# A list schedule that counts pauses on TensorE and moves 65 short runs of operations by a table

## The chip, the cores and the metric

One core of one Trainium2 chip runs the whole program. The metric is device microseconds of one execution, launch to last output; the profiler's span runs from the first to the last instruction and is a little shorter. The engines are TensorE (PE, with its weight loads as PEld), VectorE (DVE), ScalarE (ACT), GpSimd (POOL) and SyncE (SP), which here issues the weight transfers.

## What is computed

Two layers over 256 tokens of width 1024, float32 in and out, with 16 heads of 64 in 4 key groups. Each layer normalizes `x`, scales and shifts it by numbers that come from `c` through `ada_w`, runs a mixer and adds the gated result. Cut to what matters:

```
cond = silu(c)
for i in range(2):
    shift, scale, gate = split(cond @ ada_w[i] + ada_b[i], 3)
    h = rms_norm(x, norm_g[i]) * (1 + scale) + shift
    # i = 0: q, kc, vc, ks, vs, kw, vw, gates, z from h @ nsa_w_in; rms_norm and rope on q and k;
    #   p_cmp (15 compressed blocks: gelu(blocks @ cmp_w1 + b1) @ cmp_w2), p_slc, p_win (256 keys): softmax(q k) v,
    #   o = g0 * o_cmp + g1 * o_slc + g2 * o_win;  y = (o * silu(z)) @ nsa_w_out
    # i = 1: q, k, v, z from h @ moba_w_in; one causal block of 256 keys: o = softmax(q k) v
    #   y = (o * silu(z)) @ moba_w_out
    x = x + gate * y
```

## The kernel before

The program isn't issued as it is written. `T`, `A`, `V`, `G` and `S` stand for TensorE, ScalarE, VectorE, GpSimd and SyncE; every call on them is recorded by `Plan.record` with a number (its id, 2530 of them), an estimated cost (`_cost`), the operations it depends on and the buffers that it needs. At the end `Plan.issue` is a list scheduler: it keeps a clock for each engine, looks at the operations that are ready, takes the one that can start first, among equals the one of the lowest level (`FIRST_OF_ALL`, `URGENT`, `CHAIN`, `FILL`), then the one with the lowest id, and emits it. So the order on each engine, and which buffer of a tag (`ps`, `raw`, `hi`, `lo`, `p` and so on) a tile gets, are what the planner's model makes of it. Each engine then runs its own list strictly in order and waits for semaphores; the planner's clock has no part in the run itself. Since all operations are emitted from one line, nearly every row of the profile says L373 (L403 in the changed kernel), and rows are told apart by the names of their tiles.

The stages, with the times of the profile:

- To about 55 us: `condz` times `ada_w` (tiles `early`, later `raw`) gives scale and shift, columns of `h` are built (`HT`, a high and a low part in fp32r) and the key and value columns are multiplied (`acc`, `ps`).
- A weight piece of 512 KB (`raw`) is loaded by SP, cast on ACT to `hi` and subtracted on DVE to `lo`; each product is three matmuls, `hi,HT`, `lo,HT`, `hi,HT`.
- To about 100 us: query columns, the layer's gate logits (`tiny<-acc,GBIAS`, `gates`), rope on keys (`n_out`, `rot`, then `y<-n_out` and transposes `ps<-identF,y` into `KTA`), the compression (`ps<-p,p`). The z columns follow (`acc<-HT,hi`), and between them `condz` products of later `ada_w` pieces (`ps<-raw,condz`).
- 103 to 190 us: eight head pairs (`pair_a`): scores `ps<-KTA,qg`, masked maximum on DVE (`p<-ps,causal`), exponentials on ACT (`p<-p,tiny`), scaling on DVE, transposes `ps<-identF,p`, ACT copies to `pT`, values `ps<-pT,VA`, gating (`g<-zT,ps`, `qg<-g`).
- 180 to 210 us: the out projection (`hi,qg`, `lo,qg`), `x` updated, and `next_h`: sum of squares, reciprocal root (`rs`), `n_in<-X,rs`, transposes `ps<-identF,n_in`, `n_out<-ps,AB`, `HT`. The first weights of layer 1 go to `KTA`, `n_parts` and `qg` (`first_parts`).
- 210 to 258 us: layer 1's columns. To 300 us: its eight pairs (`pair_b`), among them the matmuls of the out projection. To 312 us: the rest of that projection, then the update of `x` and the output.

Groups with a `tile_position` (`values`, `ps<-p,p`, `ps<-raw,condz`) use parts of the array side by side; they are called tiled below, and a stretch of them with other matmuls on both sides is an excursion.

## Time and profile before

| | |
|---|---|
| median of 3 runs (lowest, highest) | 317.1 us (315.71, 317.89) |
| the profiled execution, its span | 317.45 us, 315.7 us |
| PE, PEld busy | 306.0 us (97%), 243.5 us (77%) |
| DVE, ACT, POOL busy | 242.2, 205.0, 26.6 us |
| DMA | 65.82 MB, mean 208 GB/s |

A row of the timeline gives the start, the time from first start to last end, engine, line, operation, output and inputs, the tile's size, how many equal instructions in a row were merged, and in brackets idle time and its releaser. Matmuls overlap, so the pace of PE is read from start to start, and a wait that is shorter than a matmul's tail shows no idle time. A row of the waits gives the waiting instruction, what it waited for, the sum, the count and the longest. A row of the stretches gives busy microseconds and instruction counts of PE, PEld, DVE, ACT and POOL, then granted clock, DMA share and GB/s.

### The profile page before, as it was taken

How to read it: one execution, taken by the hardware profiler on the slowest of the kernel's cores; microseconds unless marked ns; L12 is line 12 of the kernel's file. 1: busy time of each engine (PE TensorE's matmuls, PEld its weight loads, DVE VectorE, ACT ScalarE, POOL GpSimd, SP SyncE). 2: the span in 40 equal slices, each digit the busy share in tenths (PEclk: the TensorE clock that was granted, in tenths of full speed). 3: DMA queues.
4: the chain of work that ended last, by engine and by line, in shares of the span. 5: the costliest groups of instructions: out<-in, count | busy, mean ns of one | idle time of the engine just before them, and what ended most of it. 6: DMA issues, size and time to landing. Idle time of an engine off the chain costs nothing.

```text
span 315.7 us, 6158 instructions
## 1 busy us (share of the span) xinstructions
PE 306.0 (97%) x2133; PEld 243.5 (77%) x2133; DVE 242.2 (77%) x734; ACT 205.0 (65%) x486; POOL 26.6 (8%) x102
## 2 busy tenths in 40 slices
PE   4999999998999999999999999999999999999995
PEld 4666677777766797858879888877788999968784
DVE  4673374669982899835979887998599999999764
ACT  5735155764835787456799966786486489998420
POOL 8248900000000000000000000000000000000000
PEclk9999999999999999999999999999999999999999
DMA  7999999359899822788272377617188862423102
GB/s 248 320 357 367 368 359 323 111 171 311 279 309 306 277 79 90 246 304 250 113 261 76 116 217 226 240 60 212 65 261 263 298 229 84 155 69 120 59 34 102
DMA packets 44174, 65.82 MB, mean 208 GB/s; under 512 B 4221, under 2 KB 20971, under 8 KB 44142
## 3 DMA queue, kind: packets, MB, share of 16 engines
q1 hardware_dynamic: 43782, 65.36, 63.1%
q8 instruction: 17, 0.28, 0.4%
q14 instruction: 15, 0.12, 0.1%
q10 hardware_dynamic: 168, 0.06, 0.1%
q0 software_dynamic: 192, 0.00, 0.0%
HBM read 64.36 MB, written 1.05 MB: 207 GB/s over the span
## 4 chain that ended last, share of the span: by engine, by line
PE 90%; DMA 5%; ACT 2%; DVE 1%; issue 1%; SPq 0%; ACTq 0%; DVEq 0%
PE ps L373 54%; PE acc L373 36%; DMA raw<-in_nsa_w_in_dram 2%; DMA early<-in_ada_w_dram 2%; ACT hi L373 1%; DMA rot<-in_c_dram 0%; ACT n_in L373 0%; DVE lo L373 0%; DVE p L373 0%; ACT p L373 0%; DVE AB L373 0%; ACT HT L373 0%; DVE rot L373 0%; DVE y L373 0%; DVE X L373 0%
## 5 line engine op out<-in xcount | busy, mean ns | idle before, releaser
L373 ACT CAST hi<-raw 128x1024 fp32r<-128x1024 f32 (+1 forms) x48 | 48.8, 1023 | 25.5 <-DMA raw<-in_nsa_w_in_dram 9.8
L373 DVE TENSOR_TENSOR lo<-raw,hi 128x1024 fp32r<-128x1024 f32 (+1 forms) x48 | 56.4, 1181 | 11.0 <-ACT hi L373 10.8
L373 PE MATMUL acc<-hi,HT 128*128 128x512 f32 (+1 forms) x160 | 49.6, 381 | 1.3 <-ACT n_in L373 0.8
L373 ACT ACTIVATE p<-p,tiny 128x128 f32<-128x128 f32 (+1 forms) x96 | 43.2, 460 | 8.4 <-DVE tiny L373 8.3
L373 PE MATMUL acc<-HT,hi 128*128 128x256 f32 x192 | 37.8, 286 | 0.0
L373 PEld LDWEIGHTS acc<-hi,HT 128*128 128x128 f32 x160 | 29.1, 188 | 9.6 <-issue 2.9
L373 DVE CUSTOM_DVE_ANT_0 p<-ps,causal 128x128 f32<-128x128 f32 (+1 forms) x96 | 30.5, 346 | 3.1 <-PE ps L373 3.1
L373 PEld LDWEIGHTS acc<-HT,hi 128*128 128x128 f32 x192 | 30.1, 188 | 0.8 <-issue 0.7
L373 PE MATMUL acc<-lo,HT 128*128 128x512 f32 (+1 forms) x80 | 30.2, 380 | 0.2 <-DVE lo L373 0.2
L373 PE MATMUL ps<-hi,HT 128*128 128x512 f32 (+1 forms) x96 | 28.2, 365 | 0.0
L373 PE MATMUL acc<-HT,lo 128*128 128x256 f32 x96 | 27.8, 290 | 0.0
L373 PE MATMUL ps<-KTA,qg 128*128 128x256 f32 (+2 forms) x192 | 27.0, 284 | 0.0
L373 ACT COPY pT<-ps 128x384 f32<-128x384 f32 x48 | 21.5, 485 | 6.3 <-PE ps L373 6.2
L373 PEld LDWEIGHTS ps<-KTA,qg 128*128 128x128 f32 x192 | 24.2, 190 | 1.7 <-issue 1.2
L373 PE MATMUL ps<-hi,qg 128*128 128x256 f32 (+1 forms) x96 | 24.1, 323 | 0.0
L373 PE MATMUL acc<-hi,qg 128*128 128x512 f32 x64 | 22.8, 402 | 0.0
L373 PE MATMUL ps<-identF,p 128*128 128x128 f32 x144 | 21.7, 276 | 0.0
L373 PEld LDWEIGHTS ps<-hi,HT 128*128 128x128 f32 x96 | 17.0, 188 | 4.2 <-issue 2.1
L373 PEld LDWEIGHTS ps<-identF,p 128*128 128x128 f32 x144 | 16.4, 140 | 3.9 <-issue 1.2
L373 ACT ACTIVATION_READ_ACCUMULATOR p<-p,tiny 128x1 f32 x96 | 19.3, 201 | 0.0
L373 PE MATMUL ps<-pT,VA 128*64 128x256 f32 (+1 forms) x192 | 19.1, 334 | 0.0
L373 PEld LDWEIGHTS acc<-HT,lo 128*128 128x128 f32 x96 | 18.1, 189 | 0.1
(223 smaller groups left out, 614.5 us busy)
## 6 DMA issues: line engine op xcount, KB each, us to landing
raw<-in_ada_w_dram SPq DMA_DIRECT2D x32, 512.0 KB, 4.9
raw<-in_moba_w_in_dram SPq DMA_DIRECT2D x20, 512.0 KB, 4.3
early<-in_ada_w_dram SPq DMA_DIRECT2D x12, 512.0 KB, 9.5
raw<-in_nsa_w_in_dram SPq DMA_DIRECT2D x12, 512.0 KB, 6.4
early<-in_nsa_w_in_dram SPq DMA_DIRECT2D x9, 512.0 KB, 9.1
p<-in_nsa_cmp_w_dram SPq DMA_DIRECT2D x16, 256.0 KB, 3.8
raw<-in_nsa_w_out_dram SPq DMA_DIRECT2D x8, 512.0 KB, 5.7
raw<-in_moba_w_out_dram SPq DMA_DIRECT2D x8, 512.0 KB, 4.8
```

What stands on the lines that cost most here:

```text
L373: r = getattr(self.engines[e], method)(*[self._real(a) for a in args], **{k: self._real(a) for k, a in kw.items()})
```

## The change

Nothing of what is computed changes: the same operations are recorded with the same dependencies. What changes is the planner.

- A TensorE operation that crosses a multiple of `TICK` (10240/3 ns on the planner's clock) costs `PAUSE`, 93 ns, more.
- `_cost` counts tiled matmuls by rows as well as columns, and adds 100 ns where fewer than 128 rows are used.
- `HOLD` gives 8 ids an earliest time on the planner's clock.
- `LATER_BY` adds a number to 65 ranges of ids; the sum replaces the id as the last criterion.
- An operation that needs several new tiles of one tag is considered only when they are free together.

```
+TILED, LATER, PAUSE = -0.5, 0, 93.0
+LATER_BY = [
+    (385, 385, -73), (401, 403, 93), (413, 413, -223), (420, 422, 40), (456, 456, 66), (463, 463, -169),
...
+    (2394, 2395, -77), (2401, 2401, -45), (2407, 2407, 352),
+]
+SHIFT = {i: d for a, b, d in LATER_BY for i in range(a, b + 1)}
+HOLD = {
+    2: 800, 48: 7000, 90: 12000, 124: 17600, 247: 15900, 688: 109200, 1642: 209100, 1665: 215200,
+}
...
-                m = free(aps[1])
-                if "tile_position" in kw and m <= 64:
-                    return max(cols * 4.28 * max(32, m) / P, 60.0)
+                m, rows = free(aps[1]), aps[1].shape[0]
+                if "tile_position" in kw and m * rows <= 64 * P:
+                    return max(cols * 4.28 * max(32, m) / P * max(32, rows) / P, 60.0) + (100.0 if rows < P else 0.0)
...
-            op["at"] = 0.0
+            op["at"], op["key"] = HOLD.get(op["id"], 0.0), op["id"] + SHIFT.get(op["id"], 0)
...
+                    new = {}
+                    for n in op["needs"]:
+                        if self.tiles[n]["slot"] is None:
+                            new.setdefault(self.tiles[n]["tag"].name, []).append(n)
+                    for name, several in new.items():
+                        if len(several) > 1 and not blocked:
+                            free = sorted(self.tags[name].free)
+                            blocked = len(free) < len(several)
+                            t = t if blocked else max(t, free[len(several) - 1][0])
...
-                    found.append((t, self._rank(op, e, mode), op["id"], op))
+                    found.append((t, self._rank(op, e, mode), op["key"], op))
...
+                if (start + cost) // TICK > tick:
+                    cost += PAUSE
```

The orders that come out differ nearly everywhere: 871 of TensorE's 1278 operations stand at another place (by up to 89 places), 476 of VectorE's 638, 272 of ScalarE's 387, 40 of SyncE's 155 transfers (by up to 5), none of GpSimd's. The last 64 operations of TensorE, after 300 us, are in the old order. TensorE has 36 excursions before and 31 after. Three places, with the rows of the program's order:

**At 76 to 82 us, ScalarE and VectorE.** `n_in<-acc` copies the query columns, `tiny<-acc,GBIAS` the gate logits of the same accumulator; `hi`, `lo` are weight parts; `n_out`, `y` belong to the rope on keys. ScalarE before, then after:

```order
L373 COPY n_in_176<-acc_276 128x256
L373 ACTIVATE tiny_907<-tiny_907 128x48
L373 COPY n_in_176<-acc_283 128x256
L373 CAST hi_352<-raw_640 128x1024
L373 COPY y_143<-n_out_279 128x512
L373 COPY y_217<-n_out_279 128x512
L373 ACTIVATE tiny_925<-tiny_925 128x48
L373 ACTIVATE n_out_286<-n_in_176 128x1024
```

```order
L403 COPY n_in_182<-acc_276 128x256
L403 COPY n_in_182<-acc_288 128x256
L403 ACTIVATE tiny_911<-tiny_911 128x48
L403 ACTIVATE tiny_915<-tiny_915 128x48
L403 ACTIVATE n_out_286<-n_in_182 128x1024
L403 CAST hi_302<-raw_622 128x1024
L403 COPY y_143<-n_out_279 128x512
L403 COPY y_208<-n_out_279 128x512
```

A little ahead, at 66 to 73 us, VectorE before, then after; `lo` of 608 columns belongs to the query weights, and SP's next loads of `raw` wait for these rows:

```order
L373 TENSOR_TENSOR lo_315<-raw_625,hi_309 128x608
L373 TENSOR_REDUCE ss_819<-n_out_279 128x16
L373 TENSOR_TENSOR lo_346<-raw_640,hi_334 128x608
L373 TENSOR_SCALAR rs_834<-ss_819 128x16
L373 TENSOR_TENSOR lo_368<-raw_647,hi_352 128x608
```

```order
L403 TENSOR_TENSOR lo_369<-raw_622,hi_345 128x608
L403 TENSOR_TENSOR lo_349<-raw_636,hi_334 128x608
L403 TENSOR_REDUCE ss_835<-n_out_279 128x16
L403 TENSOR_TENSOR lo_271<-raw_644,hi_302 128x608
L403 TENSOR_SCALAR rs_853<-ss_835 128x16
```

VectorE at 75 to 79 us, before, then after:

```order
L373 TENSOR_TENSOR n_out_279<-n_in_164,TC 128x1024
L373 TENSOR_TENSOR rot_139<-n_in_164,TS 128x16x8 x2
L373 TENSOR_TENSOR tiny_907<-acc_276,GBIAS 128x48
L373 TENSOR_TENSOR lo_315<-raw_618,hi_309 128x1024
L373 TENSOR_TENSOR n_out_279<-n_out_279,rot_139 128x16x16
```

```order
L403 TENSOR_TENSOR lo_369<-raw_636,hi_345 128x1024
L403 TENSOR_TENSOR rot_140<-n_in_164,TS 128x16x8
L403 TENSOR_TENSOR tiny_911<-acc_276,GBIAS 128x48
L403 TENSOR_TENSOR rot_140<-n_in_164,TS 128x16x8
L403 TENSOR_TENSOR tiny_915<-acc_288,GBIAS 128x48
L403 TENSOR_TENSOR n_out_279<-n_in_164,TC 128x1024
```

At 66 us the second `lo` moves ahead of the reduction `ss` (on ScalarE the squares `n_out<-n_in` that it reads move behind the second cast); the third stays behind it. Later the weight part `lo` moves ahead of the gate logits and the rope product `n_out` behind them; on ScalarE the two copies `y` move from ahead of the large `n_out` to behind it, and a cast stays ahead of them.

**At 199 to 207 us, TensorE and ScalarE: the end of the first out projection and `next_h`.** ScalarE before, then after:

```order
L373 CAST hi_251<-raw_625 128x1024
L373 CAST hi_309<-raw_618 128x1024
L373 CAST hi_334<-raw_647 128x1024
L373 ACTIVATE n_in_176<-X,rs_834 128x256
L373 ACTIVATE n_out_286<-ps_162,AB_119 128x128
L373 ACTIVATE n_in_176<-X,rs_834 128x256
L373 CAST HT<-n_out_286 128x2x128
```

```order
L403 CAST hi_302<-raw_657 128x1024
L403 CAST hi_334<-raw_644 128x1024
L403 ACTIVATE n_in_182<-X,rs_853 128x256 x3
L403 ACTIVATE n_out_286<-ps_213,AB_119 128x128
L403 ACTIVATE n_out_286<-ps_162,AB_119 128x128
L403 CAST HT<-n_out_286 128x2x128 x2
```

TensorE before, then after:

```order
L373 MATMUL ps_162<-identF,n_in_176 128x128 x2
L373 MATMUL ps_212<-hi_352,qg_1448 128x512
L373 MATMUL ps_212<-lo_368,qg_1448 128x512
L373 MATMUL ps_196<-identF,n_in_176 128x128 x2
L373 MATMUL ps_212<-hi_352,qg_1448 128x512
L373 MATMUL ps_224<-identF,n_in_176 128x128 x2
L373 MATMUL acc_276<-KTA,HT 128x512 x2
```

```order
L403 MATMUL ps_213<-identF,n_in_182 128x128 x2
L403 MATMUL ps_162<-identF,n_in_182 128x128 x2
L403 MATMUL ps_233<-identF,n_in_182 128x128 x2
L403 MATMUL ps_190<-identF,n_in_182 128x128 x2
L403 MATMUL acc_276<-hi_345,qg_1504 128x512 x2
L403 MATMUL acc_276<-lo_369,qg_1504 128x512
L403 MATMUL acc_276<-hi_345,qg_1504 128x512
L403 MATMUL acc_288<-KTA,HT 128x512 x12
```

One of the three casts is no longer ahead of `n_in<-X,rs`, the three `n_in` stand together, and so do the four pairs of transposes that read them, now ahead of four matmuls of the out projection. On VectorE the subtraction `n_parts<-raw,n_parts` no longer stands between the two additions `ss<-ss` that open `next_h`.

**At 281 to 298 us, TensorE: the pairs of layer 1.** `ps<-pT,VA` is a tiled group of four calls (eight matmuls of the profile), one for each pair. Before, one of them stands between matmuls of the out projection; after, three stand in one stretch:

```order
L373 MATMUL ps_224<-hi_309,qg_1464 128x512
L373 MATMUL ps_156<-pT_1389,VA 64x256
L373 MATMUL ps_156<-pT_1275,VA 64x256
L373 MATMUL ps_156<-pT_1389,VA 64x128
L373 MATMUL ps_156<-pT_1275,VA 64x128
L373 MATMUL ps_224<-hi_309,qg_1464 128x512
```

```order
L403 MATMUL ps_233<-lo_310,qg_1510 128x512
L403 MATMUL ps_162<-pT_1275,VA 64x256
L403 MATMUL ps_162<-pT_1261,VA 64x256
...
L403 MATMUL ps_190<-pT_1239,VA 64x256
L403 MATMUL ps_190<-pT_1311,VA 64x256
...
L403 MATMUL ps_162<-pT_1269,VA 64x256
L403 MATMUL ps_162<-pT_1261,VA 64x256
...
L403 MATMUL ps_247<-KTA,qg_1545 128x256 x4
```

Further down two more groups come together, and around 272 us another two.

More of the change, by code (lines that the diff above doesn't have):

```diff
@@ L37 @@
 DEEP = 2e4
-TILED, LATER = -0.5, 0
+TILED, LATER, PAUSE = -0.5, 0, 93.0
 SHORT_ROWS, SMALL, BEHIND, EARLY_RATE = 1.1, 7e4, 5500.0, 348.0
 ISSUE, FIRST_BYTE, RATE, LANDED = 450.0, 1500.0, 315.0, 700.0
+LATER_BY = [
[12 rows of a table added]
+]
[3 more added lines that the diff above has]
+}
 class Tag:
```

10 rows, old and new, of the table LATER_BY are left out of this document.

## The prediction

> **What bounds the kernel.** I read the page first, then the waits of TensorE, then its timeline. The page:
>
> ```profile
> PE 306.0 (97%) x2133; PEld 243.5 (77%) x2133; DVE 242.2 (77%) x734; ACT 205.0 (65%) x486; POOL 26.6 (8%) x102
> PEclk9999999999999999999999999999999999999999
> PE 90%; DMA 5%; ACT 2%; DVE 1%; issue 1%; SPq 0%; ACTq 0%; DVEq 0%
> ```
>
> TensorE is busy for 97% of the span at the full granted clock, and 90% of the chain that ended last is its own. Of the waits of TensorE, three of the five longest (between the first two stands one for `x` itself):
>
> ```profile
> PE ps L373 <- POOL selP L512: 2.3, 1, 2.3
> ...
> PE acc L373 <- ACT n_in L373: 0.8, 1, 0.8
> ...
> PE ps L373 <- DVE p L373: 0.3, 1, 0.3
> ```
>
> The first and the one for `x` belong to the start, which the change hardly touches. The others shown are 1.1 us, and since a wait hides in the tail of the matmul before it, I add those that show only as a late start (below). An order of the same work can gain two things: these waits, and what TensorE loses where the kind of matmul changes. The pauses that the planner now counts come first, in a stretch of one kind:
>
> ```profile
> 228.38 0.62 PE L373 MATMUL acc<-hi,HT 128*128 128x512 f32 x2
> 229.07 0.62 PE L373 MATMUL acc<-hi,HT 128*128 128x512 f32 x2
> ...
> 234.56 0.62 PE L373 MATMUL acc<-hi,HT 128*128 128x512 f32 x2
> ```
>
> From 228.38 to 234.56 there are nine steps of three matmuls (one `lo,HT` stands between the rows). The first takes 0.69 us, and all nine take 6.18, 0.687 each. A pause of 93 ns every 3.41 us would fall on one or two of the nine and make the mean 0.01 to 0.02 longer than an undisturbed step; the first is no shorter than the mean. So counting pauses by itself is worth nothing here. Whatever the planner makes of them only reshuffles, and the time must come from the new places.
>
> [...]
>
> **Excursions.** A values group among matmuls of 512 columns:
>
> ```profile
> 288.69 0.40 PE L373 MATMUL ps<-hi,qg 128*128 128x512 f32 x1
> 289.02 0.87 PE L373 MATMUL ps<-pT,VA 128*64 128x256 f32 x8
> 289.82 0.50 PE L373 MATMUL ps<-hi,qg 128*128 128x512 f32 x1
> 290.16 0.39 PE L373 MATMUL ps<-lo,qg 128*128 128x512 f32 x1
> ```
>
> A plain step is 0.229 us (0.687 / 3 above). The step into the group (288.69 to 289.02) takes 0.33, the step after it (289.82 to 290.16) 0.34: 0.21 us for one excursion. The order has 31 instead of 36, so 5 x 0.21 = 1.05 us of TensorE work goes: one at 15 us, one around 272, three between 285 and 298. Only the last four, 0.85 us, can reach the end. The first dies at the wait that comes next.
>
> **66 to 82 us.** The longest wait after the start, in the chain in order of time, with VectorE's rows ahead of it:
>
> ```profile
> 70.08 6.94 DMA raw<-in_nsa_w_in_dram
> 77.12 1.05 ACT hi L373
> ...
> 78.49 1.65 PE acc L373 x6
> ```
>
> ```profile
> 67.99 1.22 DVE L373 TENSOR_REDUCE ss<-n_out 128x16 f32<-128x1024 f32 x1 [1.23 <-ACT n_out L373]
> 69.13 0.78 DVE L373 TENSOR_TENSOR lo<-raw,hi 128x608 fp32r<-128x608 f32 x1
> 69.91 0.79 DVE L373 TENSOR_TENSOR lo<-raw,hi 128x608 fp32r<-128x608 f32 x1
> ```
>
> The second of three loads is issued at 70.08, lands at 77.02, its cast holds ScalarE to 78.17, and only then comes the copy that frees the accumulator. TensorE waits 0.82 us. Whatever it gains before (the 0.3 us on `p`, the excursion at 15 us) ends in this wait unless the load comes earlier. After the change two things pull against each other. The first load's buffer is free earlier (its `lo` now precedes the reduction). The second load's comes later: its `lo` stands behind the reduction, whose input moved behind the second cast and a copy on ScalarE. Those two are short pieces; a cast of 1024 columns takes 1.05 us by the row at 77.12, these of 608 and 512 together about 1.2. So it ends near 71.9 instead of 70.7, and the issue slips from 70.08 by about 1.8 us. The first load then has the engines to itself and lands earlier, and 6.94 us was a load among others. The bounds for the landing are the old length, 71.9 + 6.9 = 78.8 (1.8 us late), and the page's median for loads of this size in a calmer stage:
>
> ```profile
> raw<-in_moba_w_in_dram SPq DMA_DIRECT2D x20, 512.0 KB, 4.3
> ```
>
> That is 76.2, 0.8 us early, which is about all that TensorE has to wait here. Behind it stands one thing more: the gate logits ran at 76.92 on VectorE, ahead of that copy; now `lo` (1.22 us) precedes them and they read the bank after the copy, 0.3 us later. I take 78.3 for the accumulator, 0.2 earlier than now. Then the two `y<-n_out`, behind the large `n_out` (1.05) and a cast (1.05), end near 81.7, when TensorE arrives at the transposes that read them, 78.3 + 8 x 0.23 + 1.2 for a compression pair + 0.2 = 81.6. That costs 0.1. Sum to 82 us: **-0.1**, with -0.8 and +1.8 as ends.
>
> **105 and 122 us.** The same kind of `condz` group twice:
>
> ```profile
> 105.02 1.32 PE L373 MATMUL ps<-raw,condz 128*32 128x512 f32 x8
> 106.27 0.44 PE L373 MATMUL ps<-identF,g 128*128 128x128 f32 x2
> ...
> 121.61 1.07 PE L373 MATMUL ps<-raw,condz 128*32 128x512 f32 x8
> 122.61 0.33 PE L373 MATMUL ps<-identR,n_parts 64*128 64x64 f32 x2
> ```
>
> From start to next start the first took 1.25 us, the second 1.00. I take it that the first ran while its weights were landing; it now stands directly ahead of the second, over 6 us later: **-0.25**, and nothing if the load wasn't the cause. The number of excursions stays (two groups leave a compression pair and join each other).
>
> **199 to 208 us.** ScalarE, then VectorE, then TensorE:
>
> ```profile
> 201.20 0.19 ACT L373 ACTIVATION_READ_ACCUMULATOR y<-X 128x1 f32 x1
> ...
> 204.01 1.05 ACT L373 CAST hi<-raw 128x1024 fp32r<-128x1024 f32 x1 [0.35 <-PE ps L373]
> 204.97 0.51 ACT L373 ACTIVATE n_in<-X,rs 128x256 f32<-128x256 f32 x1
> ```
>
> ```profile
> 200.77 1.22 DVE L373 TENSOR_TENSOR n_parts<-raw,n_parts 128x1024 fp32r<-128x1024 f32 x1
> 201.91 0.15 DVE L373 TENSOR_TENSOR ss<-ss 128x1 f32<-128x1 f32 x1
> ```
>
> ```profile
> 205.53 0.44 PE L373 MATMUL ps<-identF,n_in 128*128 128x128 f32 x2 [0.16 <-ACT n_in L373]
> 206.58 0.74 PE L373 MATMUL acc<-KTA,HT 128*128 128x512 f32 x2
> ```
>
> The chain of `next_h` loses two obstacles. `n_parts` no longer holds the second addition; that one then waits only for ScalarE's sum, ending at 201.39, and starts about 0.35 earlier. And the cast at 204.01 no longer stands ahead of `n_in`, so that `n_in` starts near 203.6 instead of 204.97. The first `acc<-KTA,HT` waits for the `HT` of the first chunk, which I find at 206.2 with four transposes done instead of three (0.2 us of work): 206.58 + 0.2 - 206.2 = 0.58 earlier. What is late next: ScalarE's queue of `n_out<-ps` and `HT`, and the second half's `n_in` near 214, where I count 0.1 back. **-0.5**, ends 0 and -0.8. Weight loads were also exchanged here (the first weights of layer 1 ahead of the last out weights); at my placing the last out piece is converted some 0.5 us ahead of its use, so a slip of a load there would take this term away.
>
> **240 to 300 us.** Busy time by stretch:
>
> ```profile
> 270.00:280.00 10.00, 10.00 (x82) 8.58 (x81) 9.66 (x37) 9.50 (x29) 0.00 (x0) 1.00 0.45 157
> 280.00:290.00 10.00, 10.00 (x69) 7.12 (x68) 10.00 (x41) 10.00 (x38) 0.00 (x0) 1.00 0.18 59
> 290.00:300.00 10.00, 10.00 (x66) 7.85 (x67) 7.81 (x21) 4.98 (x10) 0.00 (x0) 1.00 0.30 101
> ```
>
> VectorE works 9.66 and 10.00 of 10 us, ScalarE 9.50 and 10.00, and TensorE never waits: all three are full. Saved excursions count only if VectorE's work ahead of a values group shrinks as well. VectorE's groups from 255 to 300 us:
>
> ```profile
> L373 DVE CUSTOM_DVE_ANT_0 p<-ps,causal 128x128 f32<-128x128 f32 (+1 forms) x32 | 10.1, 345 | 0.0
> L373 DVE TENSOR_SCALAR p<-p,tiny 128x128 f32<-128x128 f32 (+1 forms) x32 | 8.2, 310 | 0.0
> L373 DVE SCALAR_TENSOR_TENSOR g<-zT,ps 128x256 f32<-128x256 f32 x8 | 3.3, 414 | 0.7 <-PE ps L373 0.7
> ```
>
> Against what VectorE had done by 284 us, its list ahead of the stretch of three groups has four maxima (`p<-ps,causal`) and seven scalings (`p<-p,tiny`) more, and six maxima, six scalings, a `g<-zT,ps` and its `qg` less. At 0.345, 0.31 and 0.41 us that is 3.6 more and 4.7 less: about 1 us shorter. So of the 0.85 us I take **-0.6**, ends 0 and -0.85. What moved behind fits where VectorE has 2.2 us to spare, 290 to 300.
>
> [...]
>
> **The sum.** -0.1 - 0.25 - 0.5 - 0.6 = -1.45. The profiled execution took 317.45 us (span 315.7), 0.35 above the median of 317.1. So 316.0 against its own time, and **315.7** against the median. Waits of 0.1 or less I leave as they are.
>
> **Rivals.** *The waits go in full.* The loads at 70 us land in about 4 us: 0.8 there, the whole 0.85 of excursions, 0.25, 0.8, and late starts that show elsewhere, such as this pair of the compression:
>
> ```profile
> 101.19 1.62 PE L373 MATMUL ps<-p,p 128*64 128x256 f32 x8
> 102.74 0.38 PE L373 MATMUL acc<-HT,hi 128*128 128x256 f32 x1
> ...
> 104.00 1.08 PE L373 MATMUL ps<-p,p 128*64 128x256 f32 x8
> ```
>
> It took 1.55 us, the next, up to 105.02, 1.02: 0.5 more. 317.1 - 3.2 = 313.9 at least, and 313.4 with a few like it. For it speaks that no engine but TensorE is full before 240 us, against it the VectorE rows.
>
> *VectorE holds the merged values groups back* (slower). Three groups in one stretch need the probabilities of three pairs, so two pairs' scalings, maxima and exponentials are wanted up to 11 us earlier. If what was put off doesn't make room, because it is needed to free `ps` or `p`, TensorE stands for those 3.6 us: 317.1 - 0.85 (the other terms) + 3.6 = 319.8. It decides from the point where VectorE's list ahead of these groups is longer than before; I count it 1 us shorter, which speaks against it.
>
> *The table's gains are the planner's alone.* Pauses that don't exist were planned around, the load at 70 us still rules, and the rest cancels: 317.1, no change.
>
> **Chances.** Forecast (314.3 to 316.6) 0.45, no change 0.22, waits in full 0.23, VectorE 0.10. I take over 1%, about what a measurement of this kernel tells from no change, as the line: faster 0.23, within it 0.67, slower 0.10. The range leaves out a tenth on either side: from 313.1, below the first rival's centre, to 318.6, which holds the +1.8 end at 78 us with the other terms at half or less.
>
> **What would show it.** A start at or below 78.3 us of the first 512-column `acc<-hi,HT` behind the 304-column ones; groups of `ps<-raw,condz` of 1.0 us at 112 us; `acc<-KTA,HT` 0.5 us earlier relative to what precedes it; 31 excursions at 0.21; no wait on VectorE in the stretch of three groups. A late landing at 77 us, or a wait on `p` or `ps` over 1 us near 285, would make it wrong.

## The result, and the profile after

The changed kernel takes **318.78 us** in the median (317.49 to 321.55), the kernel before 316.68 beside it: a ratio of **1.0071 [1.005, 1.0091]**. It is slower by 2.1 us, where 315.7 (313.1 to 318.6) was forecast, 1.45 us faster than the profiled execution of before. One of the twenty executions of before was a slow one (376.84 us) and is left out of the ratio. The profiled execution of after took 318.79 us, its span 317.1. From its page:

```profile
PE 304.9 (96%) x2133; PEld 243.6 (77%) x2133; DVE 242.6 (77%) x734; ACT 204.5 (65%) x486; POOL 28.9 (9%) x102
PEclk9999999999999999999999999999999999999999
PE 79%; DVE 8%; DMA 6%; issue 2%; ACT 2%; SPq 1%; ACTq 0%; DVEq 0%
```

TensorE is busy 1.1 us less than before, but its share of the chain that ended last falls from 90% to 79%; VectorE's grows from 1% to 8%. Four of the waits of TensorE (sum, count, longest):

```profile
PE acc L403 <- DVE tiny L403: 2.1, 1, 2.1
...
PE ps L403 <- DMA early<-in_ada_w_dram: 0.9, 2, 0.7
PE ps L403 <- DVE p L403: 0.6, 1, 0.6
PE ps L403 <- DVE n_parts L403: 0.6, 1, 0.6
```

The first stands where 0.8 us stood for `n_in`; those on `early` and `n_parts` are new, the one on `p` was 0.3. To see where the time goes I read the start of TensorE's next matmul at points where both kernels have done exactly the same work (named by the time in before; "start" is the 69th matmul):

| work done | start | 57 | 90 | 180 | 213 | 223 | 300 | last matmul |
|---|---|---|---|---|---|---|---|---|
| before | 12.93 | 56.98 | 89.65 | 180.41 | 212.83 | 223.47 | 300.29 | 311.89 |
| after | 13.39 | 56.94 | 91.59 | 182.72 | 214.56 | 224.84 | 301.68 | 313.24 |

These two executions differ by 1.35 us, less than the medians do: the one profiled of before is a late one (317.45 against 316.68), and up to 180 us profiles of the same order scatter by about a microsecond in each stretch. So I take the stretches from the profiles of all kernels below that carry the one or the other order there:

| stretch (us) | old order: mean (lowest, highest, n) | new order | difference |
|---|---|---|---|
| 0 to 57 | 56.88 (56.64, 57.22, 12) | 57.34 (56.92, 57.95, 6) | +0.46 |
| 57 to 90 | 32.73 (32.11, 33.41, 9) | 33.73 (33.05, 34.65, 4) | +1.00 |
| 90 to 180 | 90.26 (89.94, 90.76, 11) | 91.86 (91.11, 93.61, 7) | +1.60 |
| 180 to 213 | 32.41 (32.37, 32.42, 4) | 31.82 (31.79, 31.84, 5) | -0.59 |
| 213 to 223 | 10.64 (10.63, 10.64, 4) | 10.27 (10.26, 10.28, 5) | -0.37 |
| 223 to 300 | 76.83 (76.82, 76.84, 4) | 76.84 in four of five, 77.72 in one | 0 |
| 300 to the end | 11.60 (11.59, 11.60, 4) | 11.55 (11.55, 11.56, 5) | -0.05 |

The sum is +2.05 us (0.65%), which is what the medians show. The loss is made before 180 us, the gains behind it. In the three stretches ahead of 180 us the profiles of one order scatter by 0.6 to 2.5 us, so there the differences are means with a wide margin; behind 180 us they are sharp.

**66 to 80 us.** The chain of after in order of time (start, length):

```profile
67.44 3.93 DMA raw<-in_nsa_w_in_dram
...
72.22 6.36 DMA raw<-in_nsa_w_in_dram
...
78.68 1.04 ACT hi L403
79.72 0.28 ACT n_in L403
...
80.03 0.22 DVE tiny L403
...
80.29 0.73 PE acc L403 x2
```

The second load is issued at 72.22 (70.08 before), takes 6.36 us and holds ScalarE until 79.72; TensorE starts at 80.29 instead of 78.49, with 2.1 us of idle time. A part of it begins earlier, on SP's queue, first before and then after:

```profile
61.87 0.37 SPq L373 DMA_DIRECT2D raw<-in_ada_w_dram  x1
```

```profile
65.24 0.37 SPq L403 DMA_DIRECT2D raw<-in_ada_w_dram  x1
```

This load waits for a buffer that frees 3.4 us later: the subtraction `lo<-raw,hi` on VectorE that reads the buffer now stands behind four copies `p<-ps` that it stood ahead of, and runs at 64.36 instead of 61.05. Why the planner put it there isn't shown.

**256 us.** VectorE and TensorE of before, then of after:

```profile
255.23 1.28 DVE L373 TENSOR_TENSOR n_parts<-n_out,n_parts 128x512 fp32r<-128x512 f32 x2
...
255.97 1.56 PE L373 MATMUL ps<-identR,n_parts 128*128 128x128 f32 x16
```

```profile
254.75 1.22 DVE L403 TENSOR_TENSOR lo<-raw,hi 128x1024 fp32r<-128x1024 f32 x1
255.88 1.28 DVE L403 TENSOR_TENSOR n_parts<-n_out,n_parts 128x512 fp32r<-128x512 f32 x2
...
256.62 0.89 PE L403 MATMUL ps<-identR,n_parts 128*128 128x128 f32 x8 [0.62 <-DVE n_parts L403]
```

A weight part (`lo`) now stands ahead of `n_parts` on VectorE, and the group that reads it starts 0.65 us later. That takes back what the merged value groups gain behind it.

### The profile page after: what moved, and what is told of

It is laid out like the page before. It is cut to its first block, busy times and chain, and to the rows that moved or that the text cites. A ratio compares the mean times of both kernels' runs of the same rounds, so it can differ in the third digit from the quotient of the medians.

```text
span 317.1 us, 6164 instructions
## 1 busy us (share of the span) xinstructions
PE 304.9 (96%) x2133; PEld 243.6 (77%) x2133; DVE 242.6 (77%) x734; ACT 204.5 (65%) x486; POOL 28.9 (9%) x102
## 3 DMA queue, kind: packets, MB, share of 16 engines
HBM read 64.36 MB, written 1.05 MB: 206 GB/s over the span
## 4 chain that ended last, share of the span: by engine, by line
PE 79%; DVE 8%; DMA 6%; issue 2%; ACT 2%; SPq 1%; ACTq 0%; DVEq 0%
PE ps L403 48%; PE acc L403 31%; DMA raw<-in_nsa_w_in_dram 3%; DVE lo L403 3%; DMA y<-in_ada_b_dram 2%; DMA early<-in_ada_w_dram 1%; ACT hi L403 1%; DVE n_out L403 1%; DVE ss L403 1%; DVE gate L403 1%; SPq L403 1%; DVE rs L403 1%; DVE rot L403 1%; DVE p L403 1%; DVE KTA L403 0%
## 5 line engine op out<-in xcount | busy, mean ns | idle before, releaser
L403 ACT ACTIVATE p<-p,tiny 128x256 f32<-128x256 f32 (+1 forms) x96 | 42.7, 450 | 5.5 <-DVE tiny L403 5.4
L403 PE MATMUL acc<-HT,hi 128*128 128x256 f32 x192 | 39.3, 290 | 0.0
L403 DVE CUSTOM_DVE_ANT_0 p<-ps,causal 128x256 f32<-128x256 f32 (+1 forms) x96 | 30.1, 348 | 5.6 <-PE ps L403 4.9
L403 PE MATMUL ps<-KTA,qg 128*128 128x256 f32 (+2 forms) x192 | 27.8, 285 | 0.0
L403 PE MATMUL ps<-hi,qg 128*128 128x256 f32 (+1 forms) x96 | 23.3, 325 | 0.0
L403 DVE TENSOR_TENSOR lo<-early,hi 128x1024 fp32r<-128x1024 f32 (+2 forms) x17 | 17.2, 1035 | 5.4 <-ACT hi L403 5.3
L403 ACT CAST hi<-early 128x1024 fp32r<-128x1024 f32 (+2 forms) x17 | 14.7, 893 | 8.3 <-DMA early<-in_nsa_w_in_dram 6.4
L403 PE MATMUL ps<-pT,VA 128*64 128x256 f32 (+1 forms) x192 | 18.4, 333 | 0.0
```

Of the source, the lines that this page charges most:

```text
L403: r = getattr(self.engines[e], method)(*[self._real(a) for a in args], **{k: self._real(a) for k, a in kw.items()})
```

## The experiments

*Theory:* the loss is the weight loads at 67 to 72 us that wait for the late VectorE rows; what is behind them shifts as a block. *Rivals:* it lies in the eight pairs (103 to 184 us), where the order costs TensorE no visible wait; it comes of the planner's counting of pauses; it is at the start.

For orders that can be cut and joined, the planner's choice is replaced by a written list. The lists are spliced where both kernels have emitted the same set of operations (434 at 57 us, 693 at 90, 1449 at 184, 1883 at 240, 2450 at 300.5), so that the work of each piece is the same. At 184 us the sets differ by two loads of output weights, which matters below:

```
+GIVEN = [1, 2, 0, 28, 3, 13, 29, ...]      # 2530 ids
+SLOT = [-1, 0, 0, 1, ...]                  # the buffer of each tile
...
-            best = None
...
-            start, _, _, op, e = best
+            op = ops[GIVEN[done]]
+            e = op["engine"]
```

Below, `A[x:y]` stands for after's order between two of these times, `B[x:y]` for before's.

### The loads at 72 us

```
stretch_of_before   -GIVEN = A            +GIVEN = A[0:57] + B[57:90] + A[90:]
stretch_of_after    -GIVEN = B            +GIVEN = B[0:57] + A[57:90] + B[90:]
```

> The changed kernel, but from 57 to 90 us (of its profile) every engine runs the order of before; ahead of and behind that the order is that of after, operation for operation. Both kernels have done the same set of operations at both ends of this stretch, where after loses 1.8 to 1.9 us. Theory 'late load' (the loss is made in this stretch alone, by the second of the three loads of query weights): the matmul of x columns that starts at 89.65 before and 91.59 after starts at 89.6 to 89.9, the last matmul at 311.4 to 311.6 instead of 313.2, and the ratio to before is 1.0014 (1.0071 less 1.8 / 317). Rival 'spread' (the loss belongs to the whole new order, its counted pauses and merged groups): this stretch brings 0.5 us at most, ratio 1.0055 to 1.008. Rival 'given back' (a later wait takes over what is won): the gain is there at 90 us, but less than 0.9 us of it at the end, ratio 1.004 to 1.006.

> The kernel before, but from 57 to 90 us every engine runs the order of after; the rest is the order of before. Late load: 1.8 to 1.9 us lost at 90 us and nearly all of it still there at the end, ratio 1.0055 to 1.006, a little less than after, whose other stretches gain about 0.5. Spread: within 0.5 us of before, ratio 0.9995 to 1.0015. Given back: 1.8 late at 90 us, less than 0.9 at the end.

Measured: 1.0068 [1.0043, 1.0093] and 1.0033 [1.0006, 1.006]. The stretch alone makes before slower by about 1 us, but putting the old one back into after gains nothing that the medians show (the interval is 0.25% wide to either side, 0.8 us): its profile passes 90 us at 90.77 (after 91.59), and 180 us at 182.47 (182.72). This profile came 0.8 us late to 57 us (57.71, after 56.94), for a reason that the section on the start gives, so it measures the stretch less well than the medians. The theory that the rest shifts as a block isn't borne out.

Two edits of after alone at the load:

```
lo_ahead_of_sum   order of VectorE at 70 us:  -ss<-n_out, lo   +lo, ss<-n_out
                  order of ScalarE:           -n_in, n_out, hi   +hi, n_in, n_out
spare_buffer      -    plan.tag("raw", work, 1024, 5)
                  +    plan.tag("raw", work, 1024, 6)
                  +        if tag.name == "raw" and k == 5:
                  +            tag, k = self.tags["gate"], 1     # for the second load alone
```

> The changed kernel with two operations moved, and nothing else: at 68 us the third cast hi of query weights goes on ScalarE ahead of the copy n_in and the squares n_out, and its lo on VectorE ahead of the reduction ss. The buffer of the second load is so free at about 70.4 instead of 72.19. 'Issue rules' (the load takes its 6.4 us from the issue): issued at 70.6 instead of 72.22, landed at 77.0 instead of 78.58, TensorE's wait at 80.29 ends at 78.7, ratio 1.0071 less 1.6 / 317 = 1.002. 'Queues rule' (the DMA share is 1.0 from 72 to 78 us, so that a load lands when the bytes ahead of it are through): landed at 78.0 or later, the wait ends at 79.7 or later, ratio 1.005 or more. Against both, 'reduction': the sum of squares and all behind it come 0.7 us later, and if they were what TensorE waits for, the wait would end later than 80.29.

> The changed kernel in exactly its order on every engine; only the second load goes into storage that is idle at that time (the second gate buffer, unused from 45 to 127 us) and so needn't wait for the lo on VectorE. It is issued right behind the first load, at about 70.6 instead of 72.22, while cast, lo and reduction stay where they are. Issue rules: landed at 77.0, TensorE's wait at 80.29 ends at 78.7, ratio 1.002, as with the two operations moved. Queues rule: landed at 78.0 or later, wait to 79.7 or later, ratio 1.005 or more. If the place of the lo and the reduction themselves were the cause and not the load, nothing is gained: 80.29, ratio 1.007.

Measured: 1.008 [1.0052, 1.0107] and 1.008 [1.0053, 1.0108]. The mechanism is right. The timeline of TensorE in `lo_ahead_of_sum`, then those of SP and TensorE in `spare_buffer`, with the same wait on `tiny`:

```profile
78.81 0.51 PE L525 MATMUL acc<-hi,HT 128*128 128x512 f32 x1 [0.68 <-DVE tiny L525]
```

```profile
70.78 0.46 SPq L525 DMA_DIRECT2D gate<-in_nsa_w_in_dram  x1
...
79.12 0.51 PE L525 MATMUL acc<-hi,HT 128*128 128x512 f32 x1 [0.72 <-DVE tiny L525]
...
82.90 1.08 PE L525 MATMUL ps<-p,p 128*64 128x256 f32 x6 [1.08 <-DMA p<-in_nsa_cmp_w_dram]
```

An earlier issue (70.5 and 70.8 instead of 72.2) ends the wait 1.5 and 1.2 us earlier. In the second kernel the next load, of compression weights, then lands late and costs 1.08 us at 82.90. In the first the gain is there at 90 us (90.47 against 91.59) and gone at 180 us (182.66 against 182.72). So the wait at 80 us is real and can be shortened, but the median doesn't hang on it.

### The eight pairs

```
pairs_of_after     -GIVEN = B     +GIVEN = B[0:90] + A[90:184] + B[184:]
pairs_of_after_2   the same, two out-weight loads at 184 us exchanged into the order of use
pairs_of_before    -GIVEN = A     +GIVEN = A[0:90] + B[90:184] + A[184:]
```

> The kernel before, but from 90 to 184 us (the head pairs of layer 0) every engine runs the order of after. Over six profiles I took for each matmul operation its least time; what TensorE spends beyond it from 110 to 182 us is 5.1 us in the order of before and 6.2 in that of after, nearly all in steps beside a change of kind (fp32r products, fp32 transposes, other fp32 groups, tiled groups), hardly any in waits. Theory 'changes of kind': this order costs 1.1 us more wherever it starts; 184 us comes 1.0 to 1.2 later than before, the end too, ratio 1.003 to 1.0045. Rival 'late arrival': the order itself costs nothing, after was late there because it arrived late from 80 us; then 184 us is within 0.3 us of before, ratio 0.999 to 1.0015.

> Again the kernel before with the order of after from 90 to 184 us, this time with the loads and buffers at 184 us left as they are in before, so that the time behind 184 us counts too. Up to there the first try lost 1.4 us between 110 and 170 us. Changes of kind: 1.2 to 1.5 us at the last matmul against the other runs of the old order, ratio 1.004 to 1.005. Late arrival: the first try's loss came from its buffers, not from the order; within 0.3 us, ratio 0.999 to 1.0015.

> The changed kernel with the order of before from 90 to 184 us; ahead of and behind that the order of after (the load at 72 us late, as it is). If this stretch is the cause: the 1.4 to 1.5 us between 110 and 170 us are gone, the old order takes back some 0.7 of the 1.8 us late arrival at 101 to 106 us, next_h gains as in after: last matmul at 311.2 to 311.8 instead of 313.24, ratio 0.9995 to 1.003. If it only shares the loss with the late load at 80 us (each alone is enough, since a floor stands behind them): ratio 1.005 to 1.0075. Its weight loads at 184 us stand in a mixed order, so a wait on a weight part near 197 us (0.8 us in best_places) may come on top; it is read from the trace.

`pairs_of_after` (1.025) is read up to 184 us only, since behind its joint TensorE waits for weights loaded out of the order of use: 0.90 us at 199.57 and 1.06 at 201.02. There the granted clock falls to 0.50 as well, from 200.96 to 207.78, and a matmul of 512 columns takes 0.43 us instead of 0.23; from 180 to 213 us the profile takes 38.37 us instead of 32.41. With the order of use restored the ratio is **1.0073 [1.0046, 1.01]**: this stretch alone costs as much as the whole change. Its profile loses 2.85 us between 90 and 180 us against before's. `pairs_of_before` is the other way round: its stretch took 90.00 us in the profile, as with the old order elsewhere, but its median gave 1.0089 [1.0061, 1.0116]. Its profiled execution (318.18) is the fastest of its six; what the others lost isn't in a trace. A part is the joint: from 180 to 213 us the profile takes 32.84 us, where the new order otherwise takes 31.82, with waits of 0.20 us for `lo` at 197.7 and 0.33 for `n_in` at 205.7. The rest stays open, so that the old pairs mend the new order isn't shown.

No wait of TensorE stands between 105 and 180 us in either kernel. The time is in steps that are too long by less than a matmul's tail. Two groups of six transposes in after:

```profile
117.07 0.82 PE L403 MATMUL ps<-identF,p 128*128 128x128 f32 x6
117.91 0.39 PE L403 MATMUL acc<-HT,hi 128*128 128x256 f32 x1
...
162.96 0.87 PE L403 MATMUL ps<-identF,p 128*128 128x128 f32 x6
163.59 0.36 PE L403 MATMUL acc<-HT,hi 128*128 128x256 f32 x1
```

From start to next start the first takes 0.84 us, the second 0.63: 0.2 us lost, and no idle time is shown. To add up such losses, each matmul's shortest step in fifteen profiles is taken as its own. Between 110 and 170 us the old order then loses 5.3 to 5.5 us (eight profiles) and the new one 6.4 to 6.8 (seven), wherever the order starts. Nearly all of the difference is in single steps that are over 0.06 us too long: 4.1 to 4.3 us against 5.2 to 5.6. Those that end just behind a release by another engine (mostly VectorE) make 0.8 to 0.9 us of this in the old order and 1.3 to 1.8 in the new; those without one make 3.2 to 3.4 and 3.7 to 4.2. So late releases explain about half of what the new order loses here, and what makes the other steps longer stays open.

### Behind 184 us

```
tail_of_after     -GIVEN = B   +GIVEN = B[0:184] + A[184:], with one order of n_parts changed
best_places       -GIVEN = B   +GIVEN = B[0:184] + A[184:240] + B[240:260] + A[260:]
next_h_alone      -GIVEN = B   +GIVEN = B[0:184] + A[184:240] + B[240:]
tail_of_after_2   -GIVEN = B   +GIVEN = B[0:184] + A[184:]
(the last three with the two out-weight loads in the order of use)
```

> The order of before up to 184 us, that of after behind it (next_h, layer 1, the pairs with the merged groups), with one repair at 250 us: on VectorE the rope sums n_out go ahead of a weight part lo, and the two n_parts ahead of the next lo, which TensorE doesn't need for 5 us. Theory 'place by place': next_h and the first columns win 0.95 (lag 2.31 to 1.36 between 195 and 225 us), the merged groups 0.64, and the wait of 0.67 on n_parts at 256 us is gone: 1.6 us faster than before, last matmul at 310.3 against 311.9, ratio 0.995. Rival 'gains of a late start' (after wins there only because its engines and loads had 2 us more time): under 0.5 us, ratio 0.9985 to 1.001.

> The old order up to 184 us, that of after from there to 240 us (next_h, the first columns of layer 1), the old order again to 260 us, and that of after to the end (merged values groups). Place by place: next_h and the columns win 0.95, the merged groups 0.64, and the stretch at 256 us, where after waits 0.67 for n_parts, is that of before: 1.5 us faster, ratio 0.995. Rival 'gains of a late start': the gains are seen only where everything arrives 2 us late; under 0.5 us, ratio 0.9985 to 1.001.

> The kernel before with the order of after from 184 to 240 us only (the end of the first out projection, next_h, the first columns of layer 1), and the last two out-weight pieces loaded and converted in the order in which TensorE uses them, so that best_places' wait of 0.8 us at 197 us is gone. Place by place: 0.9 to 1.0 us won between 200 and 225 us and kept to the end, ratio 0.9965 to 0.998. Gains of a late start: under 0.4 us, ratio 0.999 to 1.001.

> The kernel before with the order of after from 184 us to the end, loads and buffers of the joint mended (the first try's times behind 184 us were those of its joint) and the last two out weights in the order of their use. By the places of the traces: next_h and first columns 0.95 won, 0.66 lost to n_parts at 256 us, 0.64 won by the merged groups: 0.9 us, ratio 0.9965 to 0.9985. If the merged groups gain only in a kernel that comes late: 0.3 us, ratio 0.9985 to 1.0005.

`tail_of_after` (1.035) has the same joint as above, with the granted clock at 0.50 from 197.06 to 203.88 us, and says nothing behind 184 us. `best_places`: 1.0025 [1.0004, 1.0046]; behind its joint at 240 us it waits 0.72 us for `n_parts` (255.9) and behind the one at 260 us 1.02 for `p` (264.0), so that 223 to 300 us takes 78.21 us instead of 76.83. `next_h_alone`: 0.9995 [0.9977, 1.0014]; the stretch from 180 to 233.65 takes 52.75 us against 53.24, but a new wait for `n_parts` at 254.3 (0.42 us idle) takes most of it back. `tail_of_after_2`: **0.9991 [0.9959, 1.0022]**. So everything that the change does behind 184 us together is worth nothing or a little, and the loss is ahead of it.

### The planner's rule without the table

```
no_table       -LATER_BY = [ ... ]   +LATER_BY = []      -HOLD = { ... }   +HOLD = {}
pauses_alone   (in the kernel before)
               +                if (start + cost) // TICK > tick:
               +                    cost += PAUSE
```

> The changed planner (pauses counted, the new costs of tiled matmuls, several tiles of one tag taken together) with no entry in the table and none in HOLD. If counting pauses brought something by itself, this is faster than before, ratio 0.997 or less. As I worked it out from the even steps of 0.687 us, counting them is worth nothing and only reshuffles the order: then the ratio is that of an order that nobody has chosen, 1.002 to 1.012, and the table is what brings it near to before. If the table is what does the harm, ratio 0.999 to 1.002, better than after.

> The kernel before with nothing but the counting of pauses in the planner (93 ns more for a TensorE operation that crosses a multiple of TICK); costs, table, HOLD and the rule on several tiles are left as before. The prediction says that it is worth nothing by itself and only reshuffles the order: ratio 0.997 to 1.006, whichever way the reshuffling falls. If the pauses are real and planning around them helps, 0.996 or less.

Measured: 1.0103 [1.0043, 1.0162] and 1.0095 [1.0068, 1.0122]. The rule alone makes the kernel about 1% slower; with the table it is 0.7%, and the intervals overlap, so that a gain by the table isn't shown. The places differ: `pauses_alone` takes 91.56 us from 90 to 180, like after, and loses 1.5 us more between 213 and 300; `no_table` takes 90.74 there and loses 1.9 us between 213 and 300, with waits on `HT` and `n_parts` of 1.0 each in sum.

### The start

```
head_of_after    -GIVEN = B   +GIVEN = A[0:57] + B[57:]
head_of_before   -GIVEN = A   +GIVEN = B[0:57] + A[57:]
```

> The kernel before with the order of after in the first 57 us alone (both have then done the same set of operations). If the head costs what the profiles don't show: 0.3 us at 57 us in the profile, a scatter of more than 2 us, ratio 1.003 to 1.006. If it costs nothing (the wait at 78 us and the floor at 101 us take up what comes late): within 0.3 us from 110 us on, ratio 0.999 to 1.0015.

> The changed kernel with the order of before in the first 57 us alone. If the head costs: ratio 1.001 to 1.004 instead of 1.0071, runs within 2 us. If it costs nothing: 1.005 to 1.009, as after.

Measured: 1.0028 [0.9997, 1.006] and 1.0023 [0.9992, 1.0055]. Neither differs surely from before. After with the old start is 0.48% below after by the medians, but the intervals touch. `HOLD` delays the second half of `x` past the first piece of `early` on SP's queue. The squares of that half on ScalarE, before and after:

```profile
5.53 1.06 ACT L373 ACTIVATE n_in<-X 128x1024 f32<-128x1024 f32 x1
```

```profile
7.74 1.06 ACT L403 ACTIVATE n_in<-X 128x1024 f32<-128x1024 f32 x1 [2.21 <-DMA X<-in_x_dram]
```

And TensorE breaks off for `early` behind the first two of 16 products: in all six profiles of the new start, for 0.41 to 1.12 us, and in one of the old, for 0.20. Other operations of the start have moved too, so that `HOLD` alone does it isn't shown. In after, then in `head_of_after`:

```profile
7.39 0.57 PE L403 MATMUL ps<-early,condz 128*32 128x128 f32 x2
8.65 0.64 PE L403 MATMUL ps<-early,condz 128*32 128x128 f32 x14 [0.69 <-DMA early<-in_ada_w_dram]
```

```profile
9.24 1.08 PE L525 MATMUL ps<-early,condz 128*32 128x128 f32 x14 [1.12 <-DMA early<-in_ada_w_dram]
...
11.14 1.08 PE L525 MATMUL ps<-early,condz 128*32 128x128 f32 x16
12.15 1.12 PE L525 MATMUL ps<-identF,n_in 128*128 128x128 f32 x4
```

After the longer wait the same 14 products take 1.08 us instead of 0.64, and the slow pace lasts to about 13 us. What goes with it is the record of the granted clock, which begins at 13.20 us in this trace and at 7.77 in after's (where a trace has no record, the views print 1.00, which then says nothing). With the old start the pace changes where the record begins as well, as in `no_table`, at 10.28 us:

```profile
7.84 1.08 PE L388 MATMUL ps<-early,condz 128*32 128x128 f32 x16
...
10.44 0.64 PE L388 MATMUL ps<-early,condz 128*32 128x128 f32 x16
```

In the fourteen profiles of the old start the record begins between 7.41 and 10.28 us; of the new start, between 7.35 and 7.77 in four and at 12.36 and 13.20 in two. The four pass 57 us at 57.09 in the mean, only 0.2 us behind the old start, the two at 57.83. So most of the loss at the start is made in executions whose record begins late. The length of the wait doesn't decide it: after 0.84 us (`lo_ahead_of_sum`) the 14 products took 0.64, after 0.59 (`stretch_of_before`) 1.07. Whether the wait is what makes the record begin late isn't shown by these six profiles.

### Early loads, and a version that beats both

```
tail_and_early_loads   tail_of_after + five loads one buffer earlier
best_early_loads       best_places + the same
best_of_both           next_h_alone + the same
-    plan.tag("raw", work, 1024, 5)
+    plan.tag("raw", work, 1024, 6)
...
+        if tag.name == "raw" and k == 5:
+            tag, k = self.tags["gate"], 1     # the gate buffer is idle from 53 to 82 us
```

> As the order of before with the tail of after, and five weight loads between 53 and 71 us are issued one buffer earlier: the idle second gate buffer holds the first of them (issued at 53.5 instead of 61.87), and the next four take the buffer freed one step earlier (61.87, 66.8, 69.7, 70.1 instead of 66.79, 69.66, 70.08, 70.59). The DMA share is 0.25 to 0.41 from 56 to 68 us and 0.9 to 1.0 from 68 to 106. Theory 'the stretch to 106 us waits for loads': TensorE's wait at 78.49 (0.98 with its hidden part) is gone and of the 0.8 lost at 101 to 106 on late compression weights at least half: 1.0 to 1.8 us better than the same kernel without it, ratio 0.990 to 0.992. Rival 'the queues give it back': as with the spare buffer, the compression weights p stand behind more bytes, a wait on them at 82 or 102 us takes the gain, ratio 0.994 to 0.996.

> best_places with the idle gate buffer as a sixth weight buffer between 53 and 82 us: the second condz load is issued at 53.5 instead of 61.87, the next four loads one buffer earlier each. The stretch to 106 us waits for loads: the wait at 78 us is gone and half of what is lost at 101 to 106 us, 0.6 to 1.5 us better than best_places, ratio 0.990 to 0.993. The queues give it back: the compression weights land later by as much, 82 or 102 us waits for them, and the ratio is that of best_places.

> next_h_alone with the five weight loads between 53 and 71 us one buffer earlier (as in best_early_loads). The wait at 78 us is worth what it shows: TensorE's 0.5 to 0.8 us there are gone and 0.3 to 0.8 us are left of it at 110 us, behind the floor at 101 us; ratio to before 0.994 to 0.9965, 0.1 to 0.25% below next_h_alone. If the floor behind it takes all: the ratio of next_h_alone within 0.1%.

`tail_and_early_loads` (1.0118) has the joint of `tail_of_after`, and behind 184 us some weight pieces take the place of the gate's values, so that a part of the layer's result is another one; it is read up to 180 us. `best_early_loads`: 0.9998 [0.9978, 1.0017], against 1.0025 without the loads. `best_of_both`: **0.9977 [0.9961, 0.9994]**, 315.9 us against 316.55. All its waits of TensorE behind the start:

```profile
PE acc L525 <- ACT HT L525: 0.5, 1, 0.5
PE ps L525 <- DVE n_parts L525: 0.4, 1, 0.4
PE ps L525 <- DVE p L525: 0.3, 1, 0.3
PE acc L525 <- DVE lo L525: 0.2, 1, 0.2
PE ps L525 <- DVE n_in L525: 0.2, 1, 0.2
```

The wait at 78 us is gone, and its timeline has no gap there:

```profile
77.11 0.72 PE L525 MATMUL acc<-hi,HT 128*128 128x304 f32 x2
77.67 0.40 PE L525 MATMUL acc<-lo,HT 128*128 128x512 f32 x1
```

With early loads the stretch from 57 to 90 us takes 32.03 us (31.80 to 32.18, three profiles) instead of 32.73 in the mean of the old order, whose best profile took 32.11; the one from 90 to 180 takes 90.05 to 90.35, as without them.

### What the pieces leave open

Put into before one by one, the start, 57 to 90, 90 to 184 and the rest give +0.28, +0.33, +0.73 and -0.09%, together 1.25 where the whole gives 0.71. Each has an interval of 0.25 to 0.3% to either side, so that the sum is too large isn't clear of noise. Taken out of after one by one, only the start lowers the median (from 1.0071 to 1.0023). The middle costs most when put in alone, yet taking it out alone gained nothing. Stretches ahead of 110 us seem to share a limit (a slack at 101 to 106 us that the old order has and the new one uses up); this is argued, not shown.

## Why the prediction was right or wrong

**Pauses: worth nothing by themselves.** Half right. No row shows a pause at the planned multiples: from 228.4 to 235.2 us, a stretch as long as two `TICK`, every step of TensorE takes 225 to 232 ns in before and in after. The record of the granted clock at 1.00 lasts 307.2 us in before and 310.6 in after, 90 and 91 times 3.413, and begins elsewhere in each (at 8.84 us in before, 7.77 in after, 13.20 in `head_of_after`), so a multiple counted from the program's start lies at another place in it; whether that is why no pause shows stays open. But "only reshuffles" was taken as no change, and `pauses_alone` shows 1% lost. Here a planner that reckons with a cost that no row shows didn't choose neutrally around it.

**"The start, which the change hardly touches".** This step failed: +0.46 us, made of +0.2 in the four profiles whose clock record begins early and +0.95 in the two where it begins late. `HOLD` begins with `2: 800`, the second half of `x`, and a wait for `early` of 0.41 us or more appears in every new profile. How large it came out in the mean is in part luck: with few profiles it hangs on how many had the late record.

**66 to 82 us: -0.1.** The places were right in two of three: the second load slips and `tiny` stands behind `lo`, but the first load didn't come earlier (issued at 70.11 instead of 69.66). The size failed. The issue slipped by 2.1 us (1.8 forecast), and the load landed at 78.58, by the late bound (78.8), where I had taken a value near the early one (76.2). I took an earlier issue of the first load for a relief of the second; instead the load from 61.87 moved to 65.24, and these loads fell on the same 10 us. The accumulator was free at 80.3, not 78.3. The range's end of +1.8 was met in this profile; the mean of the stretch is +1.00.

**105 and 122 us: -0.25.** Right, and a little small: the two groups now run as one,

```profile
109.55 1.93 PE L403 MATMUL ps<-raw,condz 128*32 128x512 f32 x16
111.41 0.55 PE L403 MATMUL ps<-identF,p 128*128 128x128 f32 x3
```

in 1.86 us from start to next start, where the two took 1.25 and 1.00. The gain is lost in what the same stretch loses otherwise.

**"Waits of 0.1 or less I leave as they are".** The step that failed most: 90 to 180 us costs +1.60. I counted excursions (a tiled group among plain matmuls) and waits there, found nothing beyond those two groups, and put down nothing, though 871 of TensorE's 1278 operations had moved and VectorE was busy for 19.90 and 18.00 us of 20 in two of its stretches (busy time of PE, PEld, DVE, ACT in before):

```profile
110.00:130.00 20.00, 20.00 (x167) 17.50 (x165) 19.90 (x94) 15.85 (x51) 0.00 (x0) 1.00 0.36 126
...
150.00:170.00 20.00, 20.00 (x176) 16.79 (x176) 18.00 (x97) 17.91 (x66) 0.00 (x0) 1.00 0.44 151
```

A step that is late by less than the matmul's tail shows no wait (the 0.2 us at 117.07 in after), and there are many: `pairs_of_after_2` shows that this stretch's order alone makes the kernel 0.73% slower. Late releases, most by VectorE, make about half of the added steps; the cause of the other half is open.

**`next_h`: -0.5.** Right in mechanism, too small: -0.96 from 180 to 223 us, in five of five profiles of the new order. Behind the old pairs only half of it came (-0.47 in `next_h_alone`, -0.54 in `tail_of_after_2`), so the other half hangs on what the pairs leave, which no run isolates. The four pairs of transposes stand together, and then

```profile
206.59 1.24 PE L403 MATMUL ps<-identF,n_in 128*128 128x128 f32 x8
...
208.61 3.07 PE L403 MATMUL acc<-KTA,HT 128*128 128x512 f32 x12
```

the twelve `acc<-KTA,HT` run without the break that the second half's transposes made before; where I counted 0.1 back, from 213 on, 0.37 more was gained.

**240 to 300 us: -0.6.** The merged groups gained 0.64 between 285 and 300 us, with no wait on VectorE in

```profile
287.68 2.37 PE L403 MATMUL ps<-pT,VA 128*64 128x256 f32 x24
289.98 1.61 PE L403 MATMUL ps<-KTA,qg 128*128 128x256 f32 x12
```

So VectorE didn't hold them back. But the wait on `n_parts` at 256 us, which I didn't look for, took 0.66: the term is 0.

**The frame.** I set the profiled execution 0.35 us above the median of three runs; against the median of twenty it is 0.77 above, and since the stretches behind 180 us agree within 0.05 us, that is most likely made ahead of them. A reading of a single pair of profiles would have put the change at +1.35.

## What to carry to other kernels

Where an engine is full and its order changes nearly everywhere, a sum over visible waits and excursions counts only what can be seen; steps that are too long by less than a matmul's tail need a term of their own, with a wide range (here 1.6 us over 90 us). Read two orders at points of equal work, over several executions, and place the loss before naming its cause. A removed wait is worth something only if the stretch behind it passes it on: here two edits that ended the longest wait 1.2 and 1.5 us earlier didn't lower the median, in one of them because another wait took its place.

## What the runs showed of the hardware

- Ahead of the trace's first clock record TensorE was slower: 14 products took 1.08 us in `head_of_after` at 9.24, with the first record at 13.20, and 0.64 in after at 8.65, with the first at 7.77; from start to next start they took 1.00 and 0.57. Where there is no record, the views' 1.00 isn't a measurement: before's stretches from 2 to 8 us print it, and its record begins at 8.84.
- In `pairs_of_after` two waits close together, 0.90 us at 199.57 and 1.06 at 201.02, went with a granted clock of 0.50 from 200.96 to 207.78; the single wait of 2.09 us at 80.29 in after was followed by no such fall (1.00 from 80 to 84 us).
- Of two loads of 512 KB, five microseconds apart, the one at 67.44 us took 3.93 us and the one at 72.22 took 6.36; in `spare_buffer` half as many bytes took 6.52 us at 76.34. Of these three the one of half the size took longest.
- The scatter between executions of one order is made early: in the old order 0.6 us in the stretch to 57, 1.3 from there to 90 and 0.8 to 180 (in the new one 1.0, 1.6 and 2.5), but 0.01 to 0.05 us in each stretch behind it (with one exception of 0.9, whose cause wasn't looked for). A part of it goes with the clock: of the old starts, those whose record begins by 9.0 us pass 57 us at 56.64 to 56.98, those with a later one at 56.94 to 57.22.
